# Gated linear attention on TensorE: two decay levels' products in one visit, in the halves of two banks, and the diagonal's with the states

## The chip, the cores and the metric

The kernel runs on one core of one Trainium2 chip. The time is the device time of one execution in microseconds (us), taken as the median of several runs. The profile is of one further execution; its times are counted from the first instruction of the span. The engines are TensorE (PE, with its weight loads as a row of their own, PEld), VectorE (DVE), ScalarE (ACT), GpSimd (POOL) and SyncE (SP), which here issues the loads of weights.

## What is computed

Two layers of a streaming encoder over 256 frames of width 2048. In each layer one input projection feeds three groups of heads (chunked softmax attention, gated linear attention, attention into 256 memory tokens), each group is multiplied by a SiLU gate, an output projection and a layer norm follow. The change concerns the gated linear attention (GLA) alone: 4 heads with 64 key and 128 value columns, in chunks of 64 frames.

```python
def step(state, inp):
    qc, kc, vc, gc = inp
    b = jnp.cumsum(gc, axis=1)
    decay = jnp.exp(-jnp.abs(b[:, :, None] - b[:, None, :]))
    attn = jnp.einsum('bihd,bjhd,bijhd->bhij', qc, kc, decay)
    o_intra = jnp.einsum('bhij,bjhv->bihv', attn, vc)
    o_inter = jnp.einsum('bihd,bhdv->bihv', qc * jnp.exp(b), state)
    b_last = b[:, -1]
    k_dec = kc * jnp.exp(b_last[:, None] - b)
    new_state = jnp.exp(b_last)[..., None] * state + jnp.einsum('bjhd,bjhv->bhdv', k_dec, vc)
    return new_state, o_intra + o_inter
```

The decay between two frames depends on the key column, so `attn` is not one product. The kernel splits the 64 x 64 pairs of a chunk into the diagonal (decay 1) and six levels with blocks of 32, 16, 8, 4, 2 and 1 frames. In a level, keys and queries are both multiplied with the decay to a boundary between two blocks; one product then gives the pairs that stand on opposite sides of such a boundary, and a mask picks these.

## The kernel before

Nearly all of PE's time goes to the projections. Their weights are fetched in pieces by SP, and each piece is split by `parts` (L115): ACT casts it to a rounded high part (L117, `wh`), DVE subtracts that for the low part (L118, `wl`). Four pieces can be held. A piece keeps PE busy for two to three microseconds. PE and SP run in exactly the order of the program (`manual_schedule`); the order of DVE, ACT and POOL is planned ahead of the run, with the pieces' instructions at a higher priority, and is fixed then.

After each piece the program calls `tick` (L53). The smaller computations are generators, at most two of them active. A generator runs on PE up to its next `yield n` and is due again n ticks later; each tick steps at most one that does not end. What a generator does on PE in one step is called a visit below: it stands between two pieces of a projection.

`gla` (L240) is such a generator, entered for the first time after the first piece of the third values group. Its steps, with the ticks of before:

- tick 0: two transposes (L266) of the low-rank gate columns.
- tick 2: the gate logits (L272). From these, without PE, the log gates, their running sum `b_` (L286), `kd` (L289 to L293, keys decayed to the chunk's end), and `qe` (L298, L299).
- tick 4: the diagonal, `level(-1)`. `level` (L245) takes two PSUM banks from the pool of four that all generators share (`psa`), runs 16 products of 64 x 64 by 64 columns that fill the first 256 of the 512 columns of each bank (one bank for the even heads, one for the odd), and reads each bank with one DVE instruction into `pairs`: a multiplication with `eye` for the diagonal (L259), a masked copy for the levels (L261).
- tick 8: four transposes of `kd` (L321); ACT copies the result to `kdT` (L323).
- tick 10: `decayed` (L304) for the first level, on DVE and ACT; the products that update the states (L333), in two banks `kv`, from which DVE makes the states (L341, L344). The second state product fills half of `kv[1]`, the first and third fill `kv[0]`.
- ticks 12, 15, 18, 21, 24, 27: the six levels, each followed by `decayed` for the next one.
- tick 30 and on: the products with the values and the states, the norm, transposes back.

`decayed` makes one scratch buffer with the decays (DVE, then twice ACT) and two with the decayed keys and queries (L313, L314). The scratch pool has eight buffers and is shared by all generators.

Of the kernel before, what the change touches and what calls it, by code (L numbers as in the profile page):

```python
# [22 lines left out]
CH = 64  # L23
# [4 lines left out]
LEVELS = (32, 16, 8, 4, 2, 1)  # L28
# [9 lines left out]
def hybrid_trunk_kernel(  # L38
# [50 lines left out]
    def nm(s):  # L89
        uid[0] += 1  # L90
        return f"{s}_{uid[0]}"

    def mm(o, l, r, start, stop):
        pe.matmul(o, l, r, start=start, stop=stop, skip_group_check=True)  # L94

    def bank():
        return psa.tile([P, 512], F32, name=nm("bk"), tag="bk")

    def scratch(shape, dtype=F32):
        return sc.tile(shape, dtype, name=nm("sc"), tag="sc")  # L100
# [139 lines left out]
    def gla(gw, gb, ng, gq, gk, asv, yraw):  # L240
        gqf = gq.rearrange("p b t -> p (b t)")
        gkf = gk.rearrange("p b t -> p (b t)")
        pairs = [hd.tile([P, 4, CH], F32, name=nm("pairs"), tag=f"pairs{par}") for par in range(2)]

        def level(lev, kl, ql):  # L245

            pb = [bank() for _ in range(2)]
            for t in range(2):
                for b in range(2):
                    for half in range(2):  # L250
                        for par in range(2):
                            rs = slice(par * 64, par * 64 + 64)
                            c0 = b * T + t * P + half * CH
                            mm(pb[par][half * CH:(half + 1) * CH, (t * 2 + b) * CH:(t * 2 + b + 1) * CH],
                               kl[rs, c0:c0 + CH], ql[rs, c0:c0 + CH], True, True)
            for par in range(2):
                pv = pb[par][:, :4 * CH].rearrange("p (g c) -> p g c", c=CH)
                if lev < 0:
                    dve.tensor_tensor(pairs[par], pv, eye.unsqueeze(1).to_broadcast([P, 4, CH]), op=ALU.mult)  # L259
                else:  # L260
                    dve.copy_predicated(pairs[par], lmask[:, lev].unsqueeze(1).to_broadcast([P, 4, CH]), pv)  # L261
# [35 lines left out]
        dve.tensor_copy(elast, eb.rearrange("p (g c) -> p g c", c=CH)[:, :, CH - 1])  # L297
        qe = hd.tile([P, 512], F32, name=nm("qe"), tag="qe")  # L298
        dve.tensor_tensor(qe, gqf, eb, op=ALU.mult)  # L299
        yield 2  # L300
        level(-1, gkf, gqf)
        yield 4

        def decayed(s):  # L304

            bm = b_.rearrange("p (g c) -> p g c", c=2 * s)
            dd = scratch([P, 512])
            dve.tensor_tensor(dd.rearrange("p (g c) -> p g c", c=2 * s), bm,
                              bm[:, :, s - 1:s].to_broadcast([P, 512 // (2 * s), 2 * s]), op=ALU.subtract)
            act.activation(dd, dd, AF.Abs)  # L310
            act.activation(dd, dd, AF.Exp, scale=-1.0 / 16)
            kl, ql = scratch([P, 512]), scratch([P, 512])
            dve.tensor_tensor(kl, gkf, dd, op=ALU.mult)  # L313
            dve.tensor_tensor(ql, gqf, dd, op=ALU.mult)  # L314
            return kl, ql
# [6 lines left out]
        kdT = scratch([P, 4, P])  # L322
        act.copy(kdT, pt.rearrange("p (g c) -> p g c", c=P))  # L323
        yield 2
        nxt = decayed(LEVELS[0])
        kv = [bank() for _ in range(2)]
        for c in range(3):
            rs = slice((c % 2) * 64, (c % 2) * 64 + 64)
            t = c // 2
            for b in range(2):  # L330
                for par in range(2):
                    h = 2 * b + par
                    mm(kv[c % 2][par * 64:par * 64 + 64, (t * 2 + b) * P:(t * 2 + b + 1) * P],  # L333
                       kdT[rs, t * 2 + b, par * 64:par * 64 + 64],
                       asv[rs, t, 16 + h * P:16 + (h + 1) * P], True, True)
# [9 lines left out]
                                             src[:, b], op0=ALU.mult, op1=ALU.add)  # L345
        yield 2

        for lev in range(6):
            kl, ql = nxt
            level(lev, kl, ql)  # L350
            if lev < 5:
                nxt = decayed(LEVELS[lev + 1])
                yield 3
        for par in range(2):
            for half in range(2):
                ps = slice(half * CH, (half + 1) * CH)
# [14 lines left out]
        for odd, even in ((1, 2), (3, None)):  # L371
            for b in range(2):
                for c in (odd, even):
                    if c is not None:
                        for par in range(2):
                            rs = slice(par * 64, par * 64 + 64)
                            g = (c // 2) * 2 + b
# [236 lines left out]
    for l in range(L):  # L614
# [51 lines left out]
        load_bias(0)  # L666
        load_bias(1)
        gens = [[gla(*gp, gq, gk, asv, yraw[0])]]
        waiting.extend(gens[0])
        for half in range(2):  # L670
# [34 lines left out]
        for n in range(WO_N):  # L705
            g, b = scratch([P, 512]), scratch([P, 512])
# [114 lines left out]
```

## Time and profile before

| | us |
|---|---|
| median of 3 runs | 945.02 (944.0 to 945.37) |
| profiled execution | 944.11 |
| its span | 942.3 |
| DVE busy in the span | 584.6 |
| ACT busy in the span | 497.4 |
| products of the levels (12 visits) | 8.3 |
| copies of the levels (24) | 9.3 |

A row of the timeline gives the start, the duration, the engine, the line, the operation, what is written and read, the shapes and how many such instructions are merged into the row; in brackets stands how long the engine was idle before it, and what ended that. PE's rows overlap: a product's duration runs until its last result has left the array, while the next product has long started, so the distance between starts says how long a product holds its place. Products of float32 operands appear as two rows each. A group's row gives busy time, mean duration in ns, idle time before. The rows of stretches give, after the stretch, the busy time of PE, PEld, DVE, ACT and POOL with the number of instructions, then PE's granted clock, the share of the DMA engines and GB/s.

### The profile page before, as it was taken

How to read it: one execution, taken by the hardware profiler on the slowest of the kernel's cores; microseconds unless marked ns; L12 is line 12 of the kernel's file. 1: busy time of each engine (PE TensorE's matmuls, PEld its weight loads, DVE VectorE, ACT ScalarE, POOL GpSimd, SP SyncE). 2: the span in 40 equal slices, each digit the busy share in tenths (PEclk: the TensorE clock that was granted, in tenths of full speed). 3: DMA queues.
4: the chain of work that ended last, by engine and by line, in shares of the span. 5: the costliest groups of instructions: out<-in, count | busy, mean ns of one | idle time of the engine just before them, and what ended most of it. 6: DMA issues, size and time to landing. Idle time of an engine off the chain costs nothing.

```text
span 942.3 us, 14178 instructions
## 1 busy us (share of the span) xinstructions
PE 927.4 (98%) x5506; PEld 812.6 (86%) x5506; DVE 584.6 (62%) x776; ACT 497.4 (53%) x711; POOL 30.4 (3%) x46
## 2 busy tenths in 40 slices
PE   7999999999999999999999999999999999999996
PEld 5889998898888888888878999889888888888884
DVE  5664487555555666555598545965545567566656
ACT  6554475366456665443465346644744576563340
POOL 1000000000000000000031000000000000010000
PEclk9999999999999999999999999999999999999997
DMA  8776865455555466866656465655555445676642
GB/s 267 252 273 177 298 196 167 148 186 167 191 160 162 158 188 194 255 190 193 222 187 227 142 207 177 201 161 176 156 192 173 158 156 159 200 244 205 200 134 89
DMA packets 61459, 178.75 MB, mean 190 GB/s; under 512 B 6824, under 2 KB 18376, under 8 KB 61136
## 3 DMA queue, kind: packets, MB, share of 16 engines
q1 hardware_dynamic: 59664, 173.56, 57.4%
q0 software_dynamic: 1728, 4.28, 1.9%
q8 instruction: 43, 0.70, 0.3%
q14 instruction: 24, 0.20, 0.1%
HBM read 175.69 MB, written 2.10 MB: 189 GB/s over the span
## 4 chain that ended last, share of the span: by engine, by line
PE 91%; DVE 3%; DMA 3%; issue 1%; ACT 1%; SPq 0%; DVEq 0%; ACTq 0%
PE acc L94 83%; PE bk L94 6%; DMA raw<-memT 1%; DVE wl L118 1%; DMA raw<-w 1%; PE bk L424 1%; PE bk L459 0%; DVE stats L499 0%; ACT x L117 0%; PE bk L483 0%; DVE res L518 0%; DVE res L586 0%; DVE res L498 0%; DVE res L519 0%; ACT wh L117 0%
## 5 line engine op out<-in xcount | busy, mean ns | idle before, releaser
L118 DVE TENSOR_TENSOR wl<-raw,wh 128x1024 fp32r<-128x1024 f32 (+3 forms) x325 | 378.0, 1166 | 273.7 <-ACT wh L117 268.2
L117 ACT CAST wh<-raw 128x1024 fp32r<-128x1024 f32 (+3 forms) x325 | 323.1, 995 | 348.8 <-PE acc L94 241.5
L94 PE MATMUL acc<-x,wh 128*128 128x512 f32 x1408 | 505.3, 401 | 0.0
L94 PE MATMUL acc<-x,wl 128*128 128x256 f32 x1408 | 394.7, 280 | 0.2 <-DVE wl L118 0.2
L94 PE MATMUL acc<-wh,x 128*128 128x512 f32 (+1 forms) x1120 | 322.7, 369 | 5.0 <-ACT wh L117 5.0
L94 PEld LDWEIGHTS acc<-x,wh 128*128 128x128 f32 x1408 | 264.3, 188 | 60.4 <-issue 0.3
L94 PEld LDWEIGHTS acc<-x,wl 128*128 128x128 f32 x1408 | 266.0, 189 | 0.9 <-DVE wl L118 0.5
L94 PEld LDWEIGHTS acc<-wh,x 128*128 128x128 f32 x1120 | 207.1, 189 | 31.2 <-ACT wh L117 6.4
L94 PE MATMUL acc<-wl,x 128*128 128x512 f32 (+1 forms) x560 | 206.3, 368 | 1.7 <-DVE wl L118 1.7
L94 PEld LDWEIGHTS acc<-wl,x 128*128 128x128 f32 x560 | 105.6, 189 | 14.9 <-DVE wl L118 2.9
L118 DVE TENSOR_TENSOR x<-raw,x 128x1024 fp32r<-128x1024 f32 (+2 forms) x16 | 15.3, 954 | 19.9 <-ACT x L117 19.9
L117 ACT CAST x<-raw 128x1024 fp32r<-128x1024 f32 (+2 forms) x16 | 13.4, 836 | 22.8 <-DMA raw<-memT 16.2
L416 ACT ACTIVATE sc<-sc,mx 128x128 f32<-128x128 f32 (+1 forms) x32 | 14.4, 450 | 17.8 <-DVE mx L414 17.7
L191 DVE SCALAR_TENSOR_TENSOR sc<-acc,sc 128x512 f32<-128x512 f32 x24 | 16.4, 681 | 0.0
L409 DVE SCALAR_TENSOR_TENSOR sc<-bk,bias 128x384 f32<-128x384 f32 x16 | 8.9, 554 | 10.3 <-PE bk L94 10.3
L190 ACT ACTIVATE sc<-acc 128x512 f32<-128x512 f32 x24 | 14.3, 595 | 0.0
L696 DVE TENSOR_TENSOR sc<-sc,yr 128x512 f32<-128x512 f32 x16 | 11.0, 690 | 5.2 <-ACT sc L692 5.2
L498 DVE SCALAR_TENSOR_TENSOR res<-res,acc 128x512 f32<-128x512 f32 x15 | 9.7, 684 | 7.2 <-PE acc L94 7.2
L94 PE MATMUL bk<-qk,qk 128*128 128x128 f32 (+1 forms) x64 | 13.1, 326 | 0.0
L94 PE MATMUL bk<-sc,asv 128*128 128x256 f32 (+1 forms) x64 | 13.0, 325 | 0.0
L692 ACT ACTIVATE sc<-sc 128x512 f32<-128x512 f32 x16 | 10.1, 629 | 4.6 <-DVE sc L191 4.5
L94 PEld LDWEIGHTS bk<-sc,asv 128*128 128x128 f32 x64 | 11.1, 188 | 1.5
(164 smaller groups left out, 497.6 us busy)
## 6 DMA issues: line engine op xcount, KB each, us to landing
raw<-w SPq DMA_DIRECT2D x236, 512.0 KB, 3.7
raw<-w SPq DMA_DIRECT2D x64, 388.0 KB, 3.1
raw<-w SPq DMA_DIRECT2D x39, 256.0 KB, 3.1
raw<-memT SPq DMA_DIRECT2D x6, 512.0 KB, 4.5
bias<-relw SPq DMA_DIRECT2D x16, 192.0 KB, 3.7
raw<-xT SPq DMA_DIRECT2D x4, 512.0 KB, 4.4
res<-xn SPq DMA_DIRECT2D x1, 2048.0 KB, 9.6
sc<-ln_g POOLq DMA_DIRECT2D x8, 256.0 KB, 5.3
```

What stands on the lines that cost most here:

```text
L94: pe.matmul(o, l, r, start=start, stop=stop, skip_group_check=True)
L117: act.copy(hi, src)
L118: dve.tensor_tensor(lo, src, hi.bitcast(F32), op=ALU.subtract)
L190: act.mul(dst, b, scale)
L191: dve.scalar_tensor_tensor(dst, a, scale, dst, op0=ALU.mult, op1=ALU.add)
L409: dve.scalar_tensor_tensor(s, pb[:, :384], SCALE, bias[h], op0=ALU.mult, op1=ALU.add)
L416: act.activation(s[:, own[t]], s[:, own[t]], AF.Exp, bias=mx[:, t:t + 1], accum_out=zs[:, t:t + 1])
L424: pe.transpose(pt[:, i * P:(i + 1) * P], s[:, i * P:(i + 1) * P], ident)
L498: dve.scalar_tensor_tensor(r, r, ALPHA, acc, op0=ALU.mult, op1=ALU.add)
L692: act.activation(sz, sz, AF.Silu)
L696: dve.tensor_tensor(sz, sz, yraw[i][:, j:j + 2], op=ALU.mult)
```

## The change

`level` gets its two pieces of PSUM from the caller, and works on 256 columns. Levels run in pairs: one step takes two banks, runs the first level's products into their first halves and issues its two copies, then the second level's products into the second halves and its two copies. The operands of two levels are made at once, and the next step comes six ticks later instead of three. The diagonal's step of its own disappears with its `yield 2`; its products come at the head of the states' step, half of them in a bank of their own, the others in the second half of `kv[1]`. A further `yield 2` stands ahead of the levels.

```diff
-        def level(lev, kl, ql):
-
-            pb = [bank() for _ in range(2)]
+        def level(lev, kl, ql, pb):
...
-                pv = pb[par][:, :4 * CH].rearrange("p (g c) -> p g c", c=CH)
+                pv = pb[par].rearrange("p (g c) -> p g c", c=CH)
...
         dve.tensor_tensor(qe, gqf, eb, op=ALU.mult)
-        yield 2
-        level(-1, gkf, gqf)
         yield 4
...
         act.copy(kdT, pt.rearrange("p (g c) -> p g c", c=P))
         yield 2
-        nxt = decayed(LEVELS[0])
+        nxt = [decayed(s) for s in LEVELS[:2]]
         kv = [bank() for _ in range(2)]
+        level(-1, gkf, gqf, [bank()[:, :256], kv[1][:, 256:]])
         for c in range(3):
...
         yield 2
 
-        for lev in range(6):
-            kl, ql = nxt
-            level(lev, kl, ql)
-            if lev < 5:
-                nxt = decayed(LEVELS[lev + 1])
-                yield 3
+        yield 2
+        for lev in range(0, 6, 2):
+            pb = [bank() for _ in range(2)]
+            for i, (kl, ql) in enumerate(nxt):
+                level(lev + i, kl, ql, [p[:, i * 256:(i + 1) * 256] for p in pb])
+            if lev < 4:
+                nxt = [decayed(s) for s in LEVELS[lev + 2:lev + 4]]
+                yield 6
```

The steps of `gla` then stand on ticks 0, 2, 6 (transposes of `kd`), 8 (diagonal and states), 10 (nothing on PE), 12, 18 and 24 (pairs of levels), 27 and on (the products with the values).

## The prediction

> **What bounds the kernel now.** I read the page's head and its chain first, then the groups of the gated linear attention (GLA), then the timelines of TensorE (PE), VectorE (DVE) and ScalarE (ACT) around the places where the GLA interrupts the stream of projection products ("visits").
>
> ```profile
> span 942.3 us, 14178 instructions
> PE 927.4 (98%) x5506; PEld 812.6 (86%) x5506; DVE 584.6 (62%) x776; ACT 497.4 (53%) x711; POOL 30.4 (3%) x46
> ...
> PE 91%; DVE 3%; DMA 3%; issue 1%; ACT 1%; SPq 0%; DVEq 0%; ACTq 0%
> ```
>
> PE is busy for 98% of the span and carries 91% of the chain that ended last. PE runs its program in the order written, so a microsecond that it spends on a visit, or waits in front of one, is a microsecond of the kernel; DVE at 62% and ACT at 53% have room, but only where their work is early enough.
>
> ```profile
> L261 DVE COPY_PREDICATED pairs<-lmask,bk 128x256 f32<-128x256 uint8 x24 | 9.3, 441 | 0.0
> L94 PE MATMUL bk<-sc,sc 64*64 64x64 f32 x384 | 8.3, 224 | 0.0
> ...
> L259 DVE TENSOR_TENSOR pairs<-bk,eye 128x256 f32<-128x256 f32 x4 | 1.5, 418 | 0.0
> ```
>
> 384 rows over 12 visits: a level is 32 rows on PE (16 products, each in two rows) of 224 ns. Its result is read by two DVE copies of 0.44 us, the diagonal's by two multiplications of 0.42 us.
>
> **What a merged visit saves.** The first level of layer 0, on PE:
>
> ```profile
> 144.53 0.28 PE L94 MATMUL acc<-x,wl 128*128 128x256 f32 x1
> 144.74 0.69 PE L94 MATMUL bk<-sc,sc 64*64 64x64 f32 x32
> 145.36 0.50 PE L94 MATMUL acc<-x,wh 128*128 128x512 f32 x1
> 145.69 0.28 PE L94 MATMUL acc<-x,wl 128*128 128x256 f32 x1
> 145.81 0.40 PE L94 MATMUL acc<-x,wh 128*128 128x512 f32 x1
> 146.04 0.28 PE L94 MATMUL acc<-x,wl 128*128 128x256 f32 x1
> ```
>
> A projection product with 256 columns holds its place for 0.12 us (145.69 to 145.81), one with 512 for 0.23. Without the visit the next product would start at 144.53 + 0.12 = 144.65. The level starts 0.09 later (the entry), the projection is back at 145.36, and its first product holds 0.33 instead of 0.23 (the exit). A visit costs 0.71 + 0.10 = 0.81 us. The rows themselves follow each other every (0.69 - 0.224) / 31 = 0.015 us, so 32 rows take 0.48; 0.33 is entry and exit. As the second half of a longer visit a level costs 0.48. The change removes four visits a layer (three levels joined to their neighbours, the diagonal joined to the states), eight in all: 8 x 0.33 = **2.6 us saved**. No product and no DVE or ACT instruction is removed; nothing is moved on the SP queue or POOL's.
>
> **The second half waits for the first half's copies.** This is the term that decides. In the new visit PE writes one half of two banks, DVE is to copy it, and PE's very next instruction writes the other half of the same banks. No row of before shows a product writing into a bank from which another engine has yet to read: every level takes two fresh banks and uses half of each, and every visit writes all of its bank before the read. So the price lies between nothing and the whole time until both copies are done. The copies come here:
>
> ```profile
> 145.81 1.23 DVE L118 TENSOR_TENSOR wl<-raw,wh 128x1024 fp32r<-128x1024 f32 x1
> 146.95 0.77 DVE L261 COPY_PREDICATED pairs<-lmask,bk 128x256 f32<-128x256 uint8 x2
> ...
> 164.24 1.23 DVE L118 TENSOR_TENSOR wl<-raw,wh 128x1024 fp32r<-128x1024 f32 x1 [1.60 <-ACT wh L117]
> 165.38 0.78 DVE L261 COPY_PREDICATED pairs<-lmask,bk 128x256 f32<-128x256 uint8 x2
> ...
> 181.85 0.97 DVE L118 TENSOR_TENSOR wl<-raw,wh 128x776 fp32r<-128x776 f32 x1 [0.48 <-ACT wh L117]
> 182.74 0.77 DVE L261 COPY_PREDICATED pairs<-lmask,bk 128x256 f32<-128x256 uint8 x2
> ```
> ```profile
> 163.17 0.69 PE L94 MATMUL bk<-sc,sc 64*64 64x64 f32 x32
> 181.05 0.69 PE L94 MATMUL bk<-sc,sc 64*64 64x64 f32 x32
> ```
>
> These three levels stand where the three joined visits will stand: the first level, and the ones 6 and 12 ticks later (a tick is one weight piece). In each, DVE takes the next piece's subtraction (L118) first and the two copies behind it, though at 164.24 it had sat idle for 1.60 us. DVE runs in a fixed order, so it will not step aside. The second half could start 0.48 after the first, and would start when the second copy ends, since its products alternate between the two banks. The waits: 147.72 - 145.22 = 2.50; 166.16 - 163.65 = 2.51; 183.51 - 181.53 = 1.98. That nothing waited on the copies before is why their lateness cost nothing; now PE stands behind them, and behind PE the next piece.
>
> The states' visit gets the same wait, since the second state product shares its bank with half of the diagonal.
>
> ```profile
> 131.69 0.60 PE L321 MATMUL bk<-ident,sc 128*128 128x128 f32 x4
> ...
> 137.87 1.09 PE L94 MATMUL bk<-asv,sc 64*64 64x128 f32 x24
> ```
> ```profile
> 132.89 1.23 DVE L118 TENSOR_TENSOR wl<-raw,wh 128x1024 fp32r<-128x1024 f32 x1 [0.70 <-ACT wh L117]
> ```
>
> That visit moves to the tick where the transposes now stand (131.69). The diagonal takes 0.48, the eight rows of the first state product, which write the other bank, a third of 1.09, so PE is at the shared bank at 132.53. If the subtraction of 132.89 goes first, as in the rows above, the two multiplications start 1.14 after it and take 0.75 together: 134.78. Wait: 2.25.
>
> A layer waits 2.25 + 2.50 + 2.51 + 1.98 = 9.2 us, two layers 18.5. With no subtraction ahead, the copies start as the rows end: 144.74 + 0.69 + 0.77 = 146.20, a wait of 0.98, and 0.60 for the states' visit: 3.5 a layer, 7.1 in all. With halves that may be written and read side by side: nothing. I take 18.5. The hand-over of a whole bank is what every visit in the trace does, and all three rows of DVE have the subtraction ahead.
>
> [...]
>
> **The transposes come two ticks earlier than their operand.** The diagonal's visit stood between the gates (tick 2) and the transposes of `kd` (tick 8). With it goes its `yield 2`: the transposes now stand on tick 6.
>
> ```profile
> 121.83 0.69 PE L94 MATMUL bk<-gq,gk 64*64 64x64 f32 x32
> 122.46 0.62 PE L94 MATMUL acc<-wh,x 128*128 128x388 f32 x2
> ...
> 128.91 0.39 PE L94 MATMUL acc<-x,wh 128*128 128x512 f32 x1
> ```
> ```profile
> 125.56 0.75 DVE L259 TENSOR_TENSOR pairs<-bk,eye 128x256 f32<-128x256 f32 x2
> ...
> 127.50 1.22 DVE L118 TENSOR_TENSOR wl<-raw,wh 128x1024 fp32r<-128x1024 f32 x1
> 128.63 0.69 DVE L293 TENSOR_TENSOR sc<-gk,sc 128x512 f32<-128x512 f32 x1
> ```
> ```profile
> 583.80 0.69 PE L94 MATMUL bk<-gq,gk 64*64 64x64 f32 x32
> ```
> ```profile
> 591.16 0.68 DVE L293 TENSOR_TENSOR sc<-gk,sc 128x512 f32<-128x512 f32 x1
> ```
>
> Three pieces lie between 122.46 and 128.91: 2.15 us each. Without the visit the piece at tick 4 starts at 121.83 - 0.09 = 121.74, and PE is at the transposes two pieces later, 126.0. L293, which makes `kd`, ends at 129.32; the diagonal's two multiplications (0.75), which now come later, stood ahead of it: 128.57. PE waits 2.5. In layer 1 it arrives at 588.0 and `kd` is done at 591.84 - 0.75 = 591.09: 3.1. Together **5.6**. Both move by the 1.13 of the subtraction at 127.50 if L293 goes before it (3.4 together), and by 0.75 the other way if other work takes the diagonal's place (7.1).
>
> **What costs nothing.** Two levels' operands are held at once. DVE made them long before they were needed:
>
> ```profile
> 141.78 0.68 DVE L314 TENSOR_TENSOR sc<-gq,sc 128x512 f32<-128x512 f32 x1
> ```
>
> This is the third level's operand, done 2.3 us before the first level ran at 144.74, so the first two levels' are there for the joined visit. A further pair needs six DVE operations of 0.69 in six ticks. If that cover went, a late operand would hold a visit by some 0.7. The states' visit needs three banks beside the transposes' one, which is four of four; no attention head is active yet. The last GLA visits come three ticks earlier; the heads that follow cost the same wherever they stand.
>
> **Sum.** 18.5 + 5.6 - 2.6 = +21.5 us. The profiled execution took 944.11 (span 942.3, and 1.8 around it), so 965.6 for it; it lies 0.9 below the median of three, 945.02, so about **966** beside that.
>
> **The rivals.**
> (1) Copies first. If DVE's order puts the copies ahead of the subtraction, 7.1 + 3.4 - 2.6 = +7.9: 953. For it: a new order is planned when PE depends on the copies, and DVE has idle time in front of the subtraction (1.60 at 164.24). Against it: the rows above. The forecast and this one are ends of one scale; mixtures lie between.
> (2) Halves do not wait. Then 5.6 - 2.6 = +3.0: 948. For it: the halves hold different columns. Against it: nothing in the trace does it.
> (3) Faster: only entry and exit count. The place is the boundary of a visit, the price -0.33 us each, -2.6 in all: 942.4. It decides if the waits stay under 0.33 a removed visit, so only if halves do not wait and `kd` also comes 2.5 us earlier than its row less the diagonal.
> (4) The waits also lower PE's clock. The rows of the start of a gap and of the end of the kernel:
>
> ```profile
> 480.00:484.00 4.00, 2.83 (x13) 2.20 (x13) 3.96 (x8) 1.08 (x2) 0.00 (x0) 1.00 0.41 137
> ...
> 930.00:933.00 3.00, 1.47 (x3) 0.64 (x3) 2.20 (x10) 0.29 (x1) 0.00 (x0) 0.69 0.22 87
> ...
> 936.00:939.00 3.00, 1.68 (x4) 0.76 (x3) 2.37 (x4) 0.00 (x0) 0.00 (x0) 0.50 0.62 235
> ```
>
> With 1.2 us idle in 4 the granted clock stays 1.00; with half of the time idle for 3 to 6 us it falls to 0.50. Ten waits of about 2.4 us lie between. If each gave some 3 us at half clock, 1.5 us each would be lost, 15 more: 981. [...]
>
> **How the numbers follow.** Forecast 0.58, (1) 0.22, (2) 0.07, (3) 0.06, (4) 0.05; the remaining 0.02 are small mixtures near no change. The forecast's own upper end: one more DVE operation of 0.69 ahead of each of eight copies (5.5) and 7.1 for the transposes, 944.1 + 18.5 + 5.5 + 7.1 - 2.6 = 972.6. The range goes from under (1) to a little above that, 950 to 974, and leaves out (2), (3) and (4). About 0.2% (1.9 us) is what can be told from no change here. (3) is faster by more, so 0.06; small mixtures, with a part of (2), are the 0.04 within; 0.90 slower.
>
> **What would show it.** In the changed profile the rows of a joined visit should be 32, a gap on PE ended by DVE L261, and 32 more; with 64 rows in one run, the term of 18.5 is wrong. At the shared bank a gap ended by L259. Ahead of the transposes (L321) a gap ended by L293. If subtractions no longer stand between a level's rows and its copies, (1) is right. A granted clock below 1.00 between 120 and 200 us would be (4).

## The result, and the profile after

The changed kernel takes 971.65 us (median of five, 971.12 to 975.22) against 944.63 (median of five, 943.95 to 945.37): 27.0 us more, a ratio of 1.0295 with an interval of 1.0278 to 1.0313. The profiled execution is the one of 971.65 us; its page begins and gives the chain as follows.

```profile
span 969.8 us, 14170 instructions
PE 934.4 (96%) x5506; PEld 818.1 (84%) x5506; DVE 586.6 (60%) x776; ACT 497.0 (51%) x711; POOL 30.4 (3%) x46
...
PE 85%; DVE 6%; ACT 3%; DMA 3%; issue 2%; SPq 0%; DVEq 0%; ACTq 0%
```

The work is the same: as many products, DVE and ACT instructions as before. PE's share of the chain fell from 91% to 85%, DVE's rose from 3% to 6%: PE now waits for DVE. PE's busy time rose by 7.0 us with no product added, so some products also took longer.

Who waited for whom in the changed kernel (total us, times, longest us), PE's new lines:

```profile
PE bk L94 <- DVE pairs L261: 11.0, 6, 2.0
PE bk L319 <- DVE sc L293: 5.7, 2, 3.1
...
PE bk L396 <- DVE sc L390: 3.1, 2, 1.5
...
PE bk L94 <- DVE pairs L259: 0.9, 2, 0.4
```

The three places on PE's timeline, in layer 0: the transposes of `kd`; the states' visit with the diagonal, and the first pair of levels; the last transposes of the GLA.

```profile
127.26 0.34 PE L94 MATMUL acc<-wl,x 128*128 128x388 f32 x1
130.17 1.12 PE L319 MATMUL bk<-ident,sc 128*128 128x128 f32 x4 [2.57 <-DVE sc L293]
```
```profile
137.14 0.69 PE L94 MATMUL bk<-gq,gk 64*64 64x64 f32 x32
137.65 0.61 PE L94 MATMUL bk<-asv,sc 64*64 64x128 f32 x8
138.70 0.69 PE L94 MATMUL bk<-asv,sc 64*64 64x128 f32 x16 [0.43 <-DVE pairs L259]
139.31 0.50 PE L94 MATMUL acc<-x,wh 128*128 128x512 f32 x1
...
150.61 0.69 PE L94 MATMUL bk<-sc,sc 64*64 64x64 f32 x32
153.30 1.28 PE L94 MATMUL bk<-sc,sc 64*64 64x64 f32 x32 [2.00 <-DVE pairs L261]
154.51 0.79 PE L94 MATMUL acc<-x,wh 128*128 128x512 f32 x1
```
```profile
215.24 0.33 PE L94 MATMUL acc<-wl,x 128*128 128x388 f32 x1
217.10 1.23 PE L396 MATMUL bk<-ident,sc 128*128 128x128 f32 x8 [1.53 <-DVE sc L390]
```

The pair of levels is just what was forecast in form: 32 rows, a gap ended by L261, 32 rows. The second half could have started at 150.61 + 0.48 = 151.09 and started at 153.30, a gap of 2.21. That gap is not the whole wait, since the 32 rows behind it are not one run. The second pair of layer 0, taken in short stretches so that rows that follow closely are not merged:

```profile
172.64 0.69 PE L94 MATMUL bk<-sc,sc 64*64 64x64 f32 x32
175.33 0.33 PE L94 MATMUL bk<-sc,sc 64*64 64x64 f32 x2 [2.00 <-DVE pairs L261]
175.67 0.69 PE L94 MATMUL bk<-sc,sc 64*64 64x64 f32 x30
176.28 0.50 PE L94 MATMUL acc<-x,wh 128*128 128x512 f32 x1
```
```profile
174.85 0.43 DVE L261 COPY_PREDICATED pairs<-lmask,bk 128x256 f32<-128x256 uint8 x1
175.18 0.43 DVE L261 COPY_PREDICATED pairs<-lmask,bk 128x256 f32<-128x256 uint8 x1
```

One product (two rows) goes when the first copy is done, at 175.28; the next one writes the other bank and starts when the second copy is done, at 175.61. The whole wait is read from the length of the visit: 172.64 to 176.28 is 3.64, and the same 64 rows take 1.09 where nothing holds them up (run "products first" below), so PE waits 2.55. The third pair takes 3.13 (192.73 to 195.86) and waits 2.04. The first pair waits like the second; the rest of its 3.90 (150.61 to 154.51) is clock, since PE has half of it from 153.89 on. The states' visit takes 2.17 (137.14 to 139.31) instead of 1.49 and waits 0.68.

DVE around the first pair, with the order that makes the wait long:

```profile
151.67 1.23 DVE L118 TENSOR_TENSOR wl<-raw,wh 128x1024 fp32r<-128x1024 f32 x1 [0.94 <-ACT wh L117]
152.82 0.76 DVE L261 COPY_PREDICATED pairs<-lmask,bk 128x256 f32<-128x256 uint8 x2
```

The subtraction goes ahead of the copies, as in the kernel before. The clock, by stretches (busy time of PE first, granted clock before the last two numbers):

```profile
126.59:130.00 3.41, 1.01 (x6) 0.69 (x4) 3.41 (x6) 2.71 (x4) 0.00 (x0) 1.00 0.50 148
150.48:153.89 3.41, 1.40 (x52) 1.00 (x54) 2.47 (x5) 1.04 (x1) 0.00 (x0) 1.00 0.68 222
170.96:174.37 3.41, 2.37 (x43) 1.82 (x41) 1.87 (x2) 1.04 (x1) 0.00 (x0) 1.00 0.61 189
174.37:177.79 3.42, 2.45 (x40) 2.06 (x41) 2.60 (x6) 0.00 (x0) 0.00 (x0) 1.00 0.63 207
```
```profile
130.00:133.41 3.41, 3.24 (x12) 3.24 (x13) 2.05 (x4) 1.82 (x3) 0.00 (x0) 0.50 0.74 203
153.89:157.31 3.42, 3.42 (x39) 2.91 (x30) 2.69 (x6) 1.26 (x2) 0.00 (x0) 0.50 0.56 165
```
```profile
604.00:608.00 4.00, 3.07 (x11) 3.07 (x12) 2.64 (x5) 1.84 (x4) 0.00 (x0) 0.57 0.63 219
...
628.00:632.00 4.00, 3.99 (x41) 3.36 (x42) 3.36 (x7) 1.26 (x2) 0.00 (x0) 0.57 0.50 156
```

Behind the wait for `kd` and behind the first pair of levels PE has half its clock for 3.41 us, in both layers: four stretches. The second pair of layer 0 has the same gap as the first (2.21), and its clock stays at 1.00: the gap lies across the border of two stretches, and each has PE busy for 2.4 of 3.4 us.

Summed from this trace, both layers: at the shared banks 2 x (0.68 + 2.55 + 2.55 + 2.04) = 15.6; for `kd` 2.73 + 3.29 = 6.0; for the norm 2 x 1.88 = 3.8 (a gap of 1.68, and 0.20 more in the visit, 1.54 instead of 1.34); half of the 13.0 us that PE worked at half clock (3.24, 3.42, 2.93 and 3.42 in the four stretches), 6.5, an estimate from that clock; entries and exits saved, -2.6. That is +29.3; the spans differ by 27.5. Two terms are known to be too high: the visits saved are worth 3.0 to 3.3 when measured alone, and what the norm's waits cost, 3.8, came to 2.6 alone (both below). The expectations below were worked out with the gaps alone, which gave 13.8 (0.77, 2.21, 2.21 and 1.70 a layer) for the shared banks.

### The profile page after: what moved, and what is told of

Same layout as the page of the kernel before. It is cut to its first block, busy times and chain, and to the rows that moved or that the text cites. A ratio compares the mean times of both kernels' runs of the same rounds, so it can differ in the third digit from the quotient of the medians.

```text
span 969.8 us, 14170 instructions
## 1 busy us (share of the span) xinstructions
PE 934.4 (96%) x5506; PEld 818.1 (84%) x5506; DVE 586.6 (60%) x776; ACT 497.0 (51%) x711; POOL 30.4 (3%) x46
## 4 chain that ended last, share of the span: by engine, by line
PE 85%; DVE 6%; ACT 3%; DMA 3%; issue 2%; SPq 0%; DVEq 0%; ACTq 0%
PE acc L94 77%; PE bk L94 6%; DVE wl L118 2%; DMA raw<-memT 2%; ACT wh L117 1%; DMA raw<-w 1%; ACT sc L384 1%; PE bk L425 0%; ACT x L117 0%; PE bk L460 0%; DVE stats L500 0%; DVE x L118 0%; PE bk L484 0%; DVE res L520 0%; DVE res L587 0%
## 5 line engine op out<-in xcount | busy, mean ns | idle before, releaser
L94 PE MATMUL bk<-sc,sc 64*64 64x64 f32 x384 | 10.9, 236 | 11.0 <-DVE pairs L261 11.0
L94 PEld LDWEIGHTS bk<-sc,sc 64*64 64x64 f32 x384 | 8.3, 143 | 14.2 <-DVE pairs L261 11.8
L308 ACT ACTIVATE sc<-sc 128x512 f32<-128x512 f32 x12 | 7.6, 631 | 16.7 <-DVE sc L306 13.5
```

## The experiments

Theory A takes every term of that sum at its word: PE stops in a visit because the bank it is to write has yet to be read, and the other two waits come from ticks that moved. The rivals: B, the second level's operands are late and the bank has nothing to do with it; C, the new ticks are harmless; D, entry and exit of a visit save nothing. The runs are in two groups, the first four and the last four, each on one chip beside the kernel before, whose medians there were 944.36 and 944.01. The changed kernel itself was not run again in them.

**Products first.** The changed kernel, with the DVE reads of a visit moved behind all of its products (`picked` is the second half of `level`).

```diff
+            hb = [[p[:, i * 256:(i + 1) * 256] for p in pb] for i in range(2)]
             for i, (kl, ql) in enumerate(nxt):
-                level(lev + i, kl, ql, [p[:, i * 256:(i + 1) * 256] for p in pb])
+                level(lev + i, kl, ql, hb[i])
+            for i in range(2):
+                picked(lev + i, hb[i])
...
-        level(-1, gkf, gqf, [bank()[:, :256], kv[1][:, 256:]])
+        dg = [bank()[:, :256], kv[1][:, 256:]]
+        level(-1, gkf, gqf, dg)
...
+        picked(-1, dg)
```

> The changed kernel with one thing altered: in every joined visit all products are issued first and the four DVE reads behind them; banks, halves and ticks stay. Theory A (PE waits because a bank that is still to be read may not be written): the eight gaps of PE inside the visits go (2.2, 2.2, 1.7 and 0.8 us a layer, 13.8 in all), and with them the two stretches of half clock behind the first pair of levels (3.4); 971.7 - 17.2 = 954.5. Rival B (the second level's operands are late, since two levels' are now made at once, and the copy only seems to end the gap): the gaps stay, some 971.

Measured: 952.39 (950.07 to 957.36), 19.3 us under the changed kernel. PE's timeline there:

```profile
149.32 1.16 PE L94 MATMUL bk<-sc,sc 64*64 64x64 f32 x64
150.42 0.50 PE L94 MATMUL acc<-x,wh 128*128 128x512 f32 x1
```

64 rows in one run, no gap. The operands of both levels were there, so B falls. Here the halves are shared without a wait in the visit: each bank is written wholly before it is read. The time is 2.1 us under the expectation, which had the waits too small: with 15.6 for them and 3.4 for the clock 952.6 comes out.

**Banks of their own.** The order of the change (first level, its copies, second level, its copies), but each level takes two fresh banks and leaves half of each unused.

```diff
-            pb = [bank() for _ in range(2)]
             for i, (kl, ql) in enumerate(nxt):
-                level(lev + i, kl, ql, [p[:, i * 256:(i + 1) * 256] for p in pb])
+                level(lev + i, kl, ql, [bank()[:, :256] for _ in range(2)])
...
-        level(-1, gkf, gqf, [bank()[:, :256], kv[1][:, 256:]])
+        level(-1, gkf, gqf, [bank()[:, :256], bank()[:, :256]])
```

> The changed kernel with a pair of banks for each level of a visit (four banks, half of each unused) and two banks of its own for the diagonal; order and ticks as in the change. Theory A: as if all products came first, 954 to 955, since nothing is written into a bank with an outstanding read; up to 1 us more if four banks at once delay an attention head. Rival B: 971, the gaps inside the visits stay.

Measured: 952.13 (950.76 to 953.74), the same as with products first, 19.5 us under the changed kernel, and no gap inside a visit. With the order kept and only the sharing gone, the waits are gone. So in this program it takes both, a shared bank and a read issued between two writes to it: doing away with the one took 19.5 us off, with the other 19.3. The two runs together settle the largest term. In this program a bank is also one buffer, so they do not tell whether the bank or the buffer is what may not be written yet; and no run leaves out the wait alone, so whether the engines would need it stays open.

**The ticks of before.** The changed kernel with its halves, on the ticks of before.

```diff
-        yield 4
+        yield 6
...
-
-        yield 2
         for lev in range(0, 6, 2):
...
-        yield 3
+        yield 6
```

> The changed kernel with the ticks of before: transposes of the decayed keys on 8, states on 10, pairs of levels on 12, 18, 24, products with the values on 30; the halves are shared as in the change. Theory A: the waits for the decayed keys (6.0), for the norm (3.8) and one stretch of half clock a layer (3.4) go, the waits at the shared banks stay: 971.7 - 13.2 = 958.5. Rival C (the new ticks are harmless and everything comes from the banks): stays near 970.

Measured: 962.82 (961.31 to 964.15), 8.8 us under the changed kernel and 4.3 over what was expected. No gap ahead of the transposes or of the last visit is left, so C falls. The 4.3 come in part from the norm, which was put at 3.8 and measured alone is worth 2.6 (below), and in part from the states' visit. PE and DVE there, and DVE in the changed kernel:

```profile
136.97 0.61 PE L94 MATMUL bk<-asv,sc 64*64 64x128 f32 x8
139.09 0.69 PE L94 MATMUL bk<-asv,sc 64*64 64x128 f32 x16 [1.52 <-DVE pairs L259]
```
```profile
136.48 0.69 DVE L311 TENSOR_TENSOR sc<-gk,sc 128x512 f32<-128x512 f32 x1 [0.28 <-ACT sc L309]
137.09 0.69 DVE L312 TENSOR_TENSOR sc<-gq,sc 128x512 f32<-128x512 f32 x1
137.69 0.69 DVE L306 TENSOR_TENSOR sc<-b 128x512 f32<-128x512 f32 x1
138.29 0.75 DVE L259 TENSOR_TENSOR pairs<-bk,eye 128x256 f32<-128x256 f32 x2
```
```profile
137.88 0.76 DVE L259 TENSOR_TENSOR pairs<-bk,eye 128x256 f32<-128x256 f32 x2 [1.29 <-PE bk L94]
138.56 1.22 DVE L118 TENSOR_TENSOR wl<-raw,wh 128x1024 fp32r<-128x1024 f32 x1
139.69 0.69 DVE L311 TENSOR_TENSOR sc<-gk,sc 128x512 f32<-128x512 f32 x1
```

Here DVE's order has three instructions for the levels' operands (L311, L312, L306) ahead of the diagonal's reads; in the changed kernel the same three stand behind them. The wait is 1.1 us longer a layer than in the changed kernel (idle 1.52 instead of 0.43). With other ticks DVE's order was planned anew, so a wait read from one kernel does not carry over to the next as it stands.

**The merging alone.** Products first and the ticks of before: of the change, hardly more than the four visits fewer a layer is left.

> Both: products first and the ticks of before, so that nothing is left of the change but the four visits fewer a layer. Theory A: no gaps, and each removed visit saves its entry and exit of 0.33 us: 944.6 - 2.6 = 942.0, clearly faster than before. Rival D (entry and exit are hidden in the stream, or lost again because copies of two levels come together): 944 to 946.

Measured: 941.09 (940.54 to 942.17), a ratio of 0.9966 to before (0.9952 to 0.9979); D falls. Run again in the second group, as the measure for its other kernels:

> The kernel with the merging alone once more, as the measure for the others of this call: 941 to 942.

Measured: 941.05 (940.28 to 941.95), ratio 0.9968 (0.9956 to 0.998). The two give 3.3 and 3.0 us saved, for 2.6 worked out.

```profile
145.02 1.16 PE L94 MATMUL bk<-sc,sc 64*64 64x64 f32 x64
146.11 0.50 PE L94 MATMUL acc<-x,wh 128*128 128x512 f32 x1
```

Two levels hold PE for 1.09 between entry and exit, one held it for 0.62.

**The two ticks, each alone, on the kernel with the merging alone.** First the transposes of `kd` two ticks earlier:

```diff
-        yield 6
+        yield 4
...
         yield 2
+        yield 2
+
         for lev in range(0, 6, 2):
```

> The kernel with the merging alone (products first, ticks of before), with one tick distance altered: the transposes of the decayed keys on tick 6 as in the change. Theory A: two gaps ahead of the transposes of 2.7 and 3.3 us (6.0), each with a stretch of half clock behind it where it fills a window (0 to 1.7 each): 941.1 + 6.0 + 0 to 3.4 = 947 to 950.5. Rival C (the early transposes are harmless): 941.

Measured: 950.51 (949.77 to 951.96), 9.5 us over the merging alone. The gaps are 2.57 and 3.13 us of idle time. Behind the first lies a stretch at half clock:

```profile
130.24:133.65 3.41, 3.41 (x12) 3.30 (x11) 2.05 (x4) 2.33 (x4) 0.00 (x0) 0.50 0.75 239
```

The gap of 2.57 is shorter than a stretch of 3.41, so it did not have to fill one. With a second such stretch behind the other gap, as in the changed kernel (604.45 to 607.86 at a granted clock of 0.50), 6.0 of waiting and twice 1.7 of half clock make 9.4; the 1.7 is an estimate, half of 3.41.

Then the products with the values on tick 27:

```diff
-        yield 6
+        yield 3
```

> The kernel with the merging alone, with the products with the values on tick 27 instead of 30, as in the change. Theory A: the norm's two steps then lie under shorter pieces, and the last transposes wait 1.9 us a layer: 941.1 + 3.8 = 944.9, up to 1.7 a layer more if the clock follows. Rival F (that gap in the changed kernel only came from what was late before it): 941.

Measured: 943.62 (943.03 to 945.64), 2.6 us over the merging alone, for 3.8 expected. The gap is there:

```profile
201.21 0.33 PE L94 MATMUL acc<-wl,x 128*128 128x388 f32 x1
203.07 1.23 PE L400 MATMUL bk<-ident,sc 128*128 128x128 f32 x8 [1.53 <-DVE sc L394]
```

Its cause is read from the pieces beside it, here and in the merging alone (run again):

```profile
202.24 1.29 DVE L394 TENSOR_TENSOR sc<-sc,rr 128x512 f32<-128x512 f32 x2
```
```profile
207.87 1.29 DVE L394 TENSOR_TENSOR sc<-sc,rr 128x512 f32<-128x512 f32 x2
210.26 1.04 PE L400 MATMUL bk<-ident,sc 128*128 128x128 f32 x8
```

Three ticks earlier the norm's two steps lie under pieces of 388 columns, 2.15 us each by the rows of before, where most pieces on the later ticks last 2.8. From the end of the products with the values and the states PE takes 9.6 us to the transposes (191.83 to 201.39), and DVE only begins the last multiplication for them (L394) after 10.4. In the merging alone PE takes 12.0 (198.26 to 210.26), and DVE begins after 9.6. A tick is a count of pieces and no time. Why 1.2 us less than expected is lost stays open.

**Three levels a visit.** The merging carried on, on the kernel with the merging alone: two visits of levels a layer, on ticks 12 and 24.

```diff
-        nxt = [decayed(s) for s in LEVELS[:2]]
+        nxt = [decayed(s) for s in LEVELS[:3]]
...
-        for lev in range(0, 6, 2):
-            pb = [bank() for _ in range(2)]
+        for lev in range(0, 6, 3):
+            pb = [bank() for _ in range(4)]
...
-                yield 6
+                yield 12
```

> The merging carried on: three levels a visit, two visits of levels a layer (ticks 12 and 24), products first, four banks. Theory A: one entry and exit of 0.33 us fewer a layer, 0.7 in all: 940.4. Rival G (six operands held at once fill the scratch buffers, or four banks hold up an attention head, and PE waits): 943 or more.

Measured: 940.36 (939.79 to 940.58), ratio 0.9963 (0.9951 to 0.9976), the fastest kernel of this study. Against two levels a visit it is 0.7 us less, as worked out, but the intervals of the two overlap, so the third level's share is not shown.

```profile
144.98 1.65 PE L94 MATMUL bk<-sc,sc 64*64 64x64 f32 x96
146.56 0.50 PE L94 MATMUL acc<-x,wh 128*128 128x512 f32 x1
```

96 rows, one entry, one exit. Six operands held at once left PE without a wait in these visits, so the rival G falls.

Not tried: DVE's copies ahead of the subtraction, in the kernel with shared halves.

## Why the prediction was right, and where not

Its direction and its reason were right: slower, because PE stands at the shared banks and ahead of the early transposes. Term by term:

- **Saved entries and exits, 2.6.** Measured alone 3.0 to 3.3. Right.
- **The second half waits for the first half's copies, 18.5.** That the wait hangs on the shared banks is shown (19.3 us less with products first, 19.5 with banks of their own); the trace gives 15.6. For the pairs it is right almost to the row: they wait 2.55, 2.55 and 2.04 where 2.50, 2.51 and 1.98 were worked out, the subtraction goes first, and the second half runs freely only when the second copy is done. The states' visit was priced at 2.25 and waited 0.68: the step "the subtraction of 132.89 goes first" failed. In the changed kernel DVE stood idle there for 1.29 us, took the multiplications as soon as the diagonal was done, and the subtraction after them; 0.60 had been worked out for that order.
- **The transposes wait for `kd`, 5.6.** The trace gives 6.0. Right; measured alone, it costs 9.5 because of the clock.
- **The last GLA visits three ticks earlier: nothing.** This step failed. The last transposes waited 1.88 a layer, and the three ticks cost 2.6 us when measured alone. The visits were moved under shorter pieces, and no row was looked up for what hides the norm.
- **The clock, rival (4) with a chance of 0.05.** It was put as something instead of the forecast, after ten waits and at 15 us. It came beside the forecast, after four of them, at 6.5 us (no row of before shows the 3 us at half clock that it took for each wait; the four stretches last 3.41 each), and its sign of being there (a granted clock below 1.00 between 120 and 200 us) is in the rows above. The forecast left it out and was too low by that. Its rows of before (half clock after a time half idle) would have carried a term of the sum.

So the waits of 18.5 + 5.6 were 2.5 too high, and the norm and the clock, some 10, were missing: 966 forecast, 971.65 measured. That the time lies in the range, 950 to 974, owes something to luck: its upper end stood for one more DVE operation ahead of each copy and a longer wait for `kd`, and neither came; what filled that room was the norm and the clock, which the range had not reckoned with.

Rival (1), copies first, held in one visit of four, the states'. Rivals (2) and (3) are out in this kernel; the saving of (3) is what the merging alone shows.

## What to carry to other kernels

Where two results share a PSUM bank, issue all writes into it before its first read: here that reordering of the source took 19.3 us of loss away. Where a schedule counts in pieces of other work, look up how long the pieces at the new place last, and which chain on the other engines they had hidden. Join visits to save entries and exits, worth 0.4 us a visit here (3.0 to 3.3 for eight), but first check that what they wait for is still early. And take a wait from the length of the whole visit: a merged row can hide a second stop.

## What the runs showed of the hardware

In the changed kernel PE's granted clock is 0.50 in four stretches of 3.41 us ahead of the kernel's end: from 130.00, 153.89, 604.45 and 628.34 on. The starts are 23.89, 450.56 and 23.89 us apart, 7, 132 and 7 lengths. PE was busy for 1.01, 1.40, 0.76 and 1.40 us in the stretches just before them. In the stretches from 170.96, 174.37, 191.44 and 215.33 on it was busy for 2.37, 2.45, 1.98 and 1.89, and the clock stayed at 1.00 behind them. A gap of 2.21 us was followed by half clock where it fell into one stretch (150.48 to 153.89), and not where it lay across two (170.96 to 177.79). A threshold does not come out of these figures: the first product of the kernel starts at 4.74 us, with PE idle until then, and the clock is 1.00 from the start of the span to 130.00. The stretch at half clock is a whole one, though PE is busy in it for 2.93 to 3.42 us. A product of 388 columns holds its place for 0.33 us there (131.73 to 132.06) and for 0.18 at a clock of 1.00 (126.73 to 126.91). By the clock such a stretch costs up to half of its 3.41 us, 1.7, which is an estimate.

Rows of PE overlap: the product that starts at 126.73 lasts 0.34 us, and the next one starts after 0.18. DVE's multiplication that had waited for the diagonal starts at 137.88, 0.05 us behind the end of the diagonal's rows (137.14 + 0.69).

Products first scattered more than the merging alone: the one program took 950.07 us with a mean granted clock of 0.994 and 957.36 with 0.988. These two executions have no trace, so what set them apart is not shown. The merging alone, which has no wait in its visits, stayed between 940.28 and 942.17 in all eleven executions.
